# The start of an input projection in two halves of the contraction, a helper operation on another engine, and a common raster for operand tiles

## The chip, the cores and the metric

The kernel runs on one core of one Trainium2 chip. A core has the matrix engine TensorE (PE), VectorE (DVE), ScalarE (ACT) and GpSimd (POOL), and SyncE (SP), on whose queue nearly all transfers are issued. Each engine works through its own list of instructions in order and waits where an operand or a buffer isn't ready. Operands lie in SBUF, 128 partitions wide; products are summed in PSUM, here in eight banks of 128 x 512 float32. The metric is the device time of one execution in microseconds (us); lower is better. Times of single instructions are from one profiled execution.

## The reference

A trunk of two layers over 1024 tokens of width 1024, in float32. The part in which the change moves instructions is the first step of layer 0:

```python
def rmsnorm(x, g):
    return x * lax.rsqrt(jnp.mean(x * x, axis=-1, keepdims=True) + EPS) * g

def even_mixer(hn, w_in, w_conv, g_v, w_s, b_s, w_out):
    z = hn @ w_in                       # 1024 x 1024 by 1024 x 2560
    b_gate, c_gate, x_in, u, v = jnp.split(z, [512, 1024, 1536, 2048], axis=-1)
    y_a = short_gated_conv(b_gate, c_gate, x_in, w_conv)
    y_b = chunked_spatial_gating(u, v, g_v, w_s, b_s)   # gelu(v), normed, mixed in chunks of 128
    return jnp.concatenate([y_a, y_b], axis=-1) @ w_out
...
h = h + mixer(rmsnorm(h, g_mix))                        # layer 1: latent attention and mLSTM
h = h + (silu(hn @ w_gate) * (hn @ w_up)) @ w_down      # width 2816
h = h + sigmoid(rmsnorm(h, g_ple) @ w_ple_gate) * (p @ w_ple_proj)
```

## The kernel before

**Products.** Each float32 operand is split into a high part, rounded to the matrix engine's fast float32 type (a cast on ACT), and the low rest (a subtraction on DVE). `mm3` (L186) makes a product of two such pairs by three matmuls: high by high, high by low, low by high, at L189, L190 and L191. A matmul has weights (128 x 128, loaded ahead of it) and a moving operand of 512 columns. In the rows below a name as `zv<-hzva,x0h` reads: output, moving operand, weights; h and l are high and low part.

**The start.** `load_x(0)` (L363) puts the first 512 tokens of x on SP's queue as eight tiles `xt` of 256 KB: four token groups by two quarters q of the width. `x_group(n, q, kk)` (L878) transposes one group of 128 columns by four small matmuls into a product bank (`xT`) and splits it into `x0h`, `x0l`. At L922 all eight groups of the first token half are made. Then the weights `zv_unit` of the v columns come in two parts of the contraction, `zva` and `zvb`, four tiles each, scaled by the norm's gain while they are split (L149), then the second token half of x, and `x_scale(0)` (L899): eight squares on ACT with sums (`junk`), a reciprocal root in small DVE operations (L240 to L244), and `bcast_prep` (L278), which makes two diagonal matrices `dg`, one on DVE and one on POOL. `bcast` (L295) multiplies them by ones (L298, L299) and gives R, the scale by token, to be read from `ug` (L1037) on. It is put off by `later` until two products have passed; `tick` counts them.

The loop at L984 runs over the eight token tiles of 128: a `zv` product of 24 matmuls (contraction 1024 in eight steps of three), then, after tiles 0 to 3, two `x_group` of the second token half each, after tile 3 `x_scale(1)`, after tiles 4 and 5 the transposes `ws_T`, after tile 6 the first weights `uu` of the u columns, whose raw tiles `ru` POOL multiplies by the gain (L118). `v_done` (L932) makes gelu, squares on POOL (`gvs`), a norm in small DVE operations, and the split `vh`, `vl`. The products `pu`, `pm`, `pc`, `px` and `pb` follow.

**Banks.** `B.ps` (L80) hands out six product banks in turn, `B.ps_tr` (L83) two for transposes and the like; a bank can be written again when its last reader is done.

**Pools.** SBUF tiles come from pools: const; opB (operand slots below 32); w (raw weights `raw`, six buffers, and split weights `whi`, `wlo`, eight each); tmp; and, stacked behind them, opA (operand slots from 32, `slot`, L92), whose place other pools take later in the program. In the built program the operand tiles of opB and w start at byte 64 modulo 256 of a partition, those of opA at byte 192 modulo 256.

Which products have an operand in opA: x of the first layer lies there whole, so `zv`, `pu`, `pc`, `px` and `pb` have exactly one. In `ffn_up` (L484) the moving operands `xb` of products 1 and 2 lie in slots 0 to 15; those of products 3 to 7 (`xc`) are taken from the list at L452, slots 32 to 53 first, in the order of products 6, 7, 5, 4, 3. A column runs through its products in the order 1, 6, 2, 7, 5, 4, 3, each of four pairs, 12 matmuls. In the per-layer gate (`ppg`) the slots of the second token half (`X_SLOTS`, L653) lie in opA, those of the first don't. In the down projection (`pd`) all operands lie in opB and w.

Of the kernel before, what the change touches and what calls it, by code (L numbers as in the profile page):

```python
# [11 lines left out]
F32 = mybir.dt.float32  # L12
# [9 lines left out]
P = 128  # L22
T = 1024
D = 1024
KT = D // P
NT = T // P
HT = 512
# [12 lines left out]
RAW = 6  # L40
# [6 lines left out]
class Build:  # L47
# [59 lines left out]

    def w_part(self, srcs, kt, cols, name, gcol, slots=None):
        nc = self.nc
        raw = self.wp.tile([P, kt, cols], F32, tag="raw", name=self.name(f"r{name}"), bufs=RAW)  # L110
        o = 0
        for s in srcs:
            w = s.shape[1]
            nc.sync.dma_start(raw[:, :, o : o + w], s.rearrange("(k p) c -> p k c", p=P))
            o += w
        if gcol is not None and kt > 1:
            g = self.vec[:, gcol : gcol + kt].unsqueeze(2).to_broadcast([P, kt, cols])
            nc.gpsimd.tensor_tensor(out=raw, in0=raw, in1=g, op=ALU.mult)  # L118
        if slots:
            hi, lo = (  # L120
                self.slot(i, name=f"u{name}").rearrange("p (k c) -> p k c", k=kt) for i in slots
            )
        else:
            hi = self.wp.tile([P, kt, cols], F32R, tag="whi", name=self.name(f"h{name}"), bufs=8)
            lo = self.wp.tile([P, kt, cols], F32R, tag="wlo", name=self.name(f"l{name}"), bufs=8)
        if gcol is not None and kt == 1:
            self.split_scaled(hi, lo, raw, self.vec[:, gcol : gcol + 1])
        else:
            self.split(hi, lo, raw)
        return [(hi[:, k, :], lo[:, k, :]) for k in range(kt)]  # L130
# [23 lines left out]

    def w_quarter(self, w, rows, c, name):

        t = self.wp.tile([P, 4, P], F32, tag="raw", name=self.name(f"r{name}"), bufs=RAW)
        self.nc.sync.dma_start(
            t, w[rows * HT : (rows + 1) * HT, c].rearrange("(k p) c -> p k c", p=P)
        )  # L160
        return t
# [7 lines left out]
    def w_chain(self, w, c0, c1, name, eng):  # L169


        tt = eng.tensor_tensor
        raw = lambda: self.wp.tile([P, 4, P], F32, tag="raw", name=self.name(f"s{name}"), bufs=RAW)
        a11 = self.w_quarter(w, 0, c0, name)
        a21 = self.w_quarter(w, 0, c1, name)
        a22 = self.w_quarter(w, 1, c1, name)
        a12 = self.w_quarter(w, 1, c0, name)
        s1, s2 = raw(), raw()
        tt(out=s1, in0=a21, in1=a22, op=ALU.add)
        tt(out=s2, in0=s1, in1=a11, op=ALU.subtract)  # L180
        tt(out=a21, in0=a11, in1=a21, op=ALU.subtract)
        return {1: a11, 2: a12, 4: a22, 5: s1, 6: s2, 7: a21}
# [95 lines left out]
    def bcast_prep(self, r):  # L278

        nc = self.nc  # L280
        rh = self.tp.tile([P, 4], F32R, tag="rh", name=self.name("rh"), bufs=2)
        rl = self.small("rl", (P, 4))
        nc.vector.tensor_copy(rh, r)
        nc.vector.tensor_tensor(out=rl, in0=r, in1=rh.bitcast(F32), op=ALU.subtract)
        out = []
        for i, x in enumerate((rh.bitcast(F32), rl)):
            d = self.tmp("dg", (P, 4, P), F32R)
            (nc.vector, nc.gpsimd)[i].tensor_tensor(
                out=d, in0=self.ident.unsqueeze(1).to_broadcast([P, 4, P]),
                in1=x.unsqueeze(2).to_broadcast([P, 4, P]), op=ALU.mult,  # L290
            )
            out.append(d.rearrange("p a b -> p (a b)"))
        return out
# [31 lines left out]
def trunk(ctx, tc, x, p, positions, g_mix, g_ffn, g_ple, ev_w_in, ev_w_conv, ev_g_v, ev_w_s,  # L325
          ev_b_s, ev_w_out, od_w_in, od_b_gate, od_g_qa, od_g_kva, od_w_q_up, od_w_kv_up, od_g_q,
          od_g_k, od_g_mh, od_w_out, w_gate, w_up, w_down, w_ple_proj, w_ple_gate, out):
    nc = tc.nc
# [5 lines left out]
    bp = ctx.enter_context(tc.tile_pool(name="opB", bufs=1))  # L334
    dp = ctx.enter_context(tc.tile_pool(name="dram", bufs=1, space=DRAM))
    B.wp = ctx.enter_context(tc.tile_pool(name="w", bufs=1))
    B.tp = ctx.enter_context(tc.tile_pool(name="tmp", bufs=1))

    def open_ps():
        s = ExitStack()  # L340
# [11 lines left out]

    xt = {}

    def load_x(n):
        for q in range(2):
            for j in range(4):
                t = bp.tile([P, HT], F32, tag=f"bl{n}{q * 4 + j}", name=B.name("xt"))
                r = (n * 4 + j) * P
                nc.sync.dma_start(t, x[r : r + P, q * HT : (q + 1) * HT])  # L360
                xt[n, q, j] = t

    load_x(0)  # L363

    ident = cp.tile([P, P], F32, name="ident")
    make_identity(nc, ident)
# [290 lines left out]
    def ffn_down(l, act_d, h_d, h2_d, X2, st, normed):  # L657
# [6 lines left out]

        def part(fh, ch, f, t=None):
            if t is None:
                t = B.wp.tile([P, HT], F32, tag="raw", name=B.name("rd"), bufs=RAW)
            r = (fh * half + f) * P
            nc.sync.dma_start(t, w_down[l][r : r + P, ch * HT : (ch + 1) * HT])
            return t  # L670
# [163 lines left out]
    def ple_out(l, tok, h2_d, X, r):  # L834

        pT = {}
        for n in range(2):
            pT[n] = make_pT(load_p(l, n) if n else tok, [32 + 4 * n + i for i in range(4)])
        for cg in range(2):
            c = slice(cg * HT, (cg + 1) * HT)  # L840
            grp = B.tm_load(w_ple_gate[l], [(cg * HT, (cg + 1) * HT)], f"pg{cg}")
            hs = {}
            for n in range(2):
                for j in range(4):
                    t = hs[n, j] = B.slot(n * 4 + j + 8 * cg, F32, "h2")
                    nc.sync.dma_start(t, h2_d[n][cg * 4 + j])
            wj = []
            for k in range(2):
                raw = B.wp.tile([P, HT], F32, tag="raw", name=B.name("rpj"), bufs=RAW)
                nc.sync.dma_start(raw, w_ple_proj[l][k * P : (k + 1) * P, c])  # L850
                a = B.slots2(40 + 4 * cg + 2 * k, 41 + 4 * cg + 2 * k, "wj")
                B.split(a[0], a[1], raw)
                wj.append(a)
            for tt in range(NT):
                n, t = tt // 4, slice((tt % 4) * P, (tt % 4 + 1) * P)
                pg = B.tm_mm(grp, X, tt, "ppg")
                pj = B.ps("ppj")
                for k in range(2):
                    a = pT[n][k]
                    B.mm3(pj, (a[0][:, t], a[1][:, t]), wj[k], k == 0, k == 1)  # L860
                ph = B.ps_tr("ph")
                for j in range(4):
                    nc.tensor.transpose(ph[:, j * P : (j + 1) * P], hs[n, j][:, t], ident)
                s = B.tmp("psg")
                nc.scalar.activation(s, pg, AF.Sigmoid, scale=r[n][:, tt % 4 : tt % 4 + 1])
                nc.vector.tensor_tensor(out=s, in0=pj, in1=s, op=ALU.mult)
                nc.vector.tensor_tensor(out=s, in0=ph, in1=s, op=ALU.add)
                nc.sync.dma_start(out[tt * P : (tt + 1) * P, c], s)
# [30 lines left out]
    def x_scale(n):  # L899
        ss = B.small("ss", (P, 4, 2))  # L900
        for q in range(2):
            for j in range(4):
                junk = B.tmp("junk")
                nc.scalar.activation(
                    junk, xt[n, q, j], AF.Square, accum_out=ss[:, j, q : q + 1]
                )
        s4 = B.small("s4", (P, 4))
        nc.vector.tensor_tensor(out=s4, in0=ss[:, :, 0], in1=ss[:, :, 1], op=ALU.add)
        r = B.tp.tile([P, 4], F32, tag=f"rt{n}", name=B.name("rt"), bufs=2)
        B.tok_rms(s4, D, r)  # L910
        rtok[n] = r
        dg = B.bcast_prep(r)

        def fn():
            R[n] = B.bcast(n, dg)

        B.later(2, fn)

    pv = B.ps_tr("pvec", (P, 16))
    nc.tensor.transpose(pv, rows0, ident[0:16, 0:16])  # L920
    nc.vector.tensor_copy(vec[:, 0:16], pv)
    for q in range(2):  # L922
        for kk in range(4):
            x_group(0, q, kk)
    zv_unit = B.w_unit(w_in[0:512, 2048:2560], 4, HT, "zva", G_MIX)
    zv_unit += B.w_unit(w_in[512:1024, 2048:2560], 4, HT, "zvb", G_MIX + 4)
    load_x(1)
    x_scale(0)

    vch = {}  # L930

# [49 lines left out]
        w_in[:, 1536 + pr * P : 1536 + (pr + 1) * P], KT, P, f"u{pr}", G_MIX, slots  # L981
    )

    for tt in range(NT):  # L984
        ps = B.tm_mm((zv_unit, HT), X, tt, "zv")
        if tt == 1:
            pv = B.ps_tr("pvec", (P, 80))
            nc.tensor.transpose(pv, rows, ident[0:80, 0:80])
            nc.vector.tensor_copy(vec[:, 16:80], pv[:, 16:80])
        if tt < 4:  # L990
            for kk in range(2):
                x_group(1, tt // 2, (tt % 2) * 2 + kk)
            if tt == 3:
                x_scale(1)
        elif tt < 6:
            ws_T(tt - 4)
        elif tt == 6:
            u0 = u_unit(0, ((28, 29), (30, 31)))
        v_done(tt, ps)

# [241 lines left out]
    def up_weights(src, kt, cols, gcol, name):  # L1242
        pairs = []
        half = cols // 2
        for k in range(kt):
# [2 lines left out]
            )  # L1248
            for i in range(2):
                c = slice(i * half, (i + 1) * half)  # L1250
                raw = B.wp.tile([P, half], F32, tag="raw", name=B.name(f"r{name}"), bufs=RAW)
                nc.sync.dma_start(raw, src[k * P : (k + 1) * P, c])
                B.split_scaled(t[0][:, c], t[1][:, c], raw, col(gcol + k))
            pairs.append(t)
# [690 lines left out]
```

## Time and profile before

| what | value |
|---|---|
| time, median of 3 runs (lowest, highest) | 2453.76 us (2452.49, 2454.29) |
| profiled execution: its time, its span | 2453.51 us, 2451.8 us |
| busy in the span: PE, DVE, ACT, POOL | 98%, 64%, 40%, 28% |
| first `zv` product, first `pu` product start | 14.99 us, 73.39 us |

The span runs from the first to the last recorded instruction; 1.7 us of the execution's time lie around it. An engine's busy share says little of the end by itself: an idle stretch counts only where the matrix engine waits in it.

### The profile page before, as it was taken

What the parts mean: (1) busy time and instruction counts of PE and PEld (TensorE: products, weight loads), DVE (VectorE), ACT (ScalarE), POOL (GpSimd) and SP (SyncE); (2) the same over time, 40 slices, a digit from 0 to 9 for tenths busy, and PEclk for the clock granted to TensorE, in tenths of its full rate; (3) what the DMA queues carried; (4) which work ended last, traced back from release to release, by engine and by line L of the source; (5) the groups of instructions that cost most, each with busy time, mean ns of one, the idle gap of its engine ahead of it and who ended that gap; (6) DMA issues with size and microseconds to landing.
All of it is one profiled execution on the core that took longest, in us unless ns stands there. A gap on an engine that the chain in (4) does not pass through costs nothing.

```text
span 2451.8 us, 33875 instructions
## 1 busy us (share of the span) xinstructions
PE 2413.6 (98%) x11510; PEld 1993.8 (81%) x11510; DVE 1561.2 (64%) x3079; ACT 988.2 (40%) x1877; POOL 679.8 (28%) x678
## 2 busy tenths in 40 slices
PE   7999999999999999999999999999999999999999
PEld 6878887788888888888888788878788888888877
DVE  6864479645556778776785566548855455687731
ACT  5322244233233545444554455635333232454520
POOL 3452121546553000112321132111256556100000
PEclk9999999999999999999999999999999999999999
DMA  4221453433236966553454843154433233886721
GB/s 151 78 86 48 136 169 101 141 99 112 91 108 204 308 226 214 174 173 96 114 154 121 228 112 106 46 168 134 129 120 112 87 111 103 286 281 210 251 97 39
DMA packets 358685, 350.74 MB, mean 143 GB/s; under 512 B 24011, under 2 KB 249648, under 8 KB 358512
## 3 DMA queue, kind: packets, MB, share of 16 engines
q1 hardware_dynamic: 358016, 348.25, 45.3%
q8 instruction: 90, 1.47, 0.2%
q0 software_dynamic: 464, 0.33, 0.1%
q14 instruction: 83, 0.68, 0.1%
q10 hardware_dynamic: 32, 0.01, 0.0%
HBM read 255.18 MB, written 93.32 MB: 142 GB/s over the span
## 4 chain that ended last, share of the span: by engine, by line
PE 52%; DVE 4%; issue 2%; DMA 1%; ACT 1%; POOL 0%; SPq 0%; DVEq 0%; POOLq 0%; ACTq 0%
PE p L190 5%; PE p L189 5%; PE p L191 5%; PE pd L189 3%; PE pd L190 3%; PE pd L191 3%; PE O L1833 2%; PE ppg L191 2%; PE ppg L190 2%; PE ppg L189 2%; PE PT L1875 1%; PE po L189 1%; PE po L190 1%; PE po L191 1%; PE S L1775 1%
## 5 line engine op out<-in xcount | busy, mean ns | idle before, releaser
L189 PE MATMUL pd<-acth,hd 128*128 128x512 f32 x616 | 240.0, 390 | 0.1
L190 PE MATMUL pd<-actl,hd 128*128 128x512 f32 x616 | 239.7, 389 | 0.0
L191 PE MATMUL pd<-acth,ld 128*128 128x512 f32 x616 | 239.7, 389 | 0.0
L189 PE MATMUL p<-xch,hg 128*128 128x512 f32 x440 | 173.1, 394 | 5.3 <-DVE sg L534 2.2
L190 PE MATMUL p<-xcl,hg 128*128 128x512 f32 x440 | 173.1, 393 | 0.2
L189 PE MATMUL p<-xch,hu 128*128 128x512 f32 x440 | 173.0, 393 | 0.0
L191 PE MATMUL p<-xch,lu 128*128 128x512 f32 x440 | 172.9, 393 | 0.0
L191 PE MATMUL p<-xch,lg 128*128 128x512 f32 x440 | 172.9, 393 | 0.0
L190 PE MATMUL p<-xcl,hu 128*128 128x512 f32 x440 | 172.6, 392 | 0.0
L541 POOL TENSOR_TENSOR act<-act,sg 128x512 f32<-128x512 f32 x60 | 90.0, 1499 | 244.1 <-DVE act L534 239.3
L146 ACT CAST hu<-ru 128x512 fp32r<-128x512 f32 x116 | 71.6, 622 | 183.3 <-PE p L190 170.4
L189 PEld LDWEIGHTS pd<-acth,hd 128*128 128x128 f32 x616 | 115.6, 188 | 24.3 <-DVE res L728 0.5
L191 PEld LDWEIGHTS pd<-acth,ld 128*128 128x128 f32 x616 | 115.6, 188 | 24.3
L146 ACT CAST hg<-rg 128x512 fp32r<-128x512 f32 x110 | 68.2, 620 | 165.9 <-PE p L190 135.6
L190 PEld LDWEIGHTS pd<-actl,hd 128*128 128x128 f32 x616 | 115.6, 188 | 23.8
L147 DVE TENSOR_TENSOR lu<-ru,hu 128x512 fp32r<-128x512 f32 x116 | 117.2, 1011 | 14.9 <-ACT hu L146 14.9
L146 ACT CAST hd<-rd 128x512 fp32r<-128x512 f32 x110 | 68.3, 621 | 133.5 <-PE pd L190 82.2
L147 DVE TENSOR_TENSOR actl<-ra,acth 128x512 fp32r<-128x512 f32 x154 | 109.5, 712 | 12.1 <-ACT acth L146 12.0
L259 POOL TENSOR_TENSOR S<-S,sq 128x512 f32<-128x512 f32 x38 | 51.6, 1359 | 219.7 <-ACT sq L257 219.7
L147 DVE TENSOR_TENSOR ld<-rd,hd 128x512 fp32r<-128x512 f32 x110 | 76.9, 699 | 47.6 <-ACT hd L146 47.6
L189 PEld LDWEIGHTS p<-xch,hg 128*128 128x128 f32 x440 | 82.6, 188 | 26.5 <-ACT hg L146 3.0
L146 ACT CAST acth<-ra 128x512 fp32r<-128x512 f32 x154 | 94.7, 616 | 13.1 <-DMA ra<-act 9.3
(561 smaller groups left out, 6615.9 us busy)
## 6 DMA issues: line engine op xcount, KB each, us to landing
ra<-act SPq DMA_DIRECT2D x154, 256.0 KB, 3.7
rd<-in_w_down SPq DMA_DIRECT2D x154, 256.0 KB, 4.0
rg<-in_w_gate SPq DMA_DIRECT2D x100, 256.0 KB, 3.3
ru<-in_w_up SPq DMA_DIRECT2D x100, 256.0 KB, 2.9
act<-act SPq DMA_DIRECT2D x88, 256.0 KB, 2.0
act<-at SPq DMA_DIRECT2D x66, 256.0 KB, 2.0
rpg<-in_w_ple_gate SPq DMA_DIRECT2D x48, 256.0 KB, 3.0
sd<-in_w_down SPq DMA_DIRECT2D x44, 256.0 KB, 4.2
```

What stands on the lines that cost most here:

```text
L146: self.nc.scalar.copy(hi, src)
L147: (eng or self.nc.vector).tensor_tensor(out=lo, in0=src, in1=hi.bitcast(F32), op=ALU.subtract)
L189: mm(ps, a[0], b[0], start=first, stop=False, skip_group_check=more)
L190: mm(ps, a[0], b[1], start=False, stop=False, skip_group_check=more)
L191: mm(ps, a[1], b[0], start=False, stop=last, skip_group_check=more)
L259: eng.tensor_tensor(out=st[n], in0=st[n], in1=sq, op=ALU.add)
L541: (nc.vector if last else nc.gpsimd).tensor_tensor(out=t, in0=t, in1=sg[d["i"], key], op=ALU.mult)
L1775: mm(s[:, 0:w], q0, K0[:, c0 : c0 + w], start=True, stop=False)
L1833: nc.tensor.matmul(O[h][:, b * DV : (b + 1) * DV], t[:, j * P : (j + 1) * P], V[h // 2][:, kb, (h % 2) * DV : (h % 2 + 1) * DV], start=kb ...
L1875: nc.tensor.transpose(pt[:, j * P : (j + 1) * P], e[:, j * P : (j + 1) * P], ident)
```

## The change

Three things. First, x and the first weights are loaded in quarters and the first products are made in two parts. `load_x` takes the quarters to load; the queue gets the first quarter of x, `zva`, the second quarter, `zvb`. Four product banks are opened at once, and for token tiles 0 to 3 the first half of the contraction (12 matmuls) is made before the second; the transposes of x's second quarter stand after the first halves of tiles 1 and 2. `x_scale(0)` comes behind the first halves, and R four products later instead of two. The transposes of the second token half stand, four groups each, after tiles 1 and 2 instead of two groups after each of tiles 0 to 3; `ws_T` and the first u weights come one tile later. Second, both diagonals of `bcast_prep` are made by DVE; there are ten calls in the program. Third, the raw tiles get a pool of their own, and this and tmp are put on the right side of SBUF. In the built program the operand tiles of opA then start at byte 64 modulo 256, as those of opB and w, which stay at 64.

```diff
-    B.tp = ctx.enter_context(tc.tile_pool(name="tmp", bufs=1))
+    B.rp = ctx.enter_context(tc.tile_pool(name="raw", bufs=1, side="right"))
+    B.tp = ctx.enter_context(tc.tile_pool(name="tmp", bufs=1, side="right"))
...
-        raw = self.wp.tile([P, kt, cols], F32, tag="raw", name=self.name(f"r{name}"), bufs=RAW)
+        raw = self.rp.tile([P, kt, cols], F32, tag="raw", name=self.name(f"r{name}"), bufs=RAW)
...
-        for i, x in enumerate((rh.bitcast(F32), rl)):
+        for x in (rh.bitcast(F32), rl):
             d = self.tmp("dg", (P, 4, P), F32R)
-            (nc.vector, nc.gpsimd)[i].tensor_tensor(
+            nc.vector.tensor_tensor(
...
-    def load_x(n):
-        for q in range(2):
+    def load_x(n, qs=(0, 1)):
+        for q in qs:
...
-    load_x(0)
+    load_x(0, (0,))
...
-        B.later(2, fn)
+        B.later(4, fn)
...
-    for q in range(2):
-        for kk in range(4):
-            x_group(0, q, kk)
+    for kk in range(4):
+        x_group(0, 0, kk)
     zv_unit = B.w_unit(w_in[0:512, 2048:2560], 4, HT, "zva", G_MIX)
+    load_x(0, (1,))
     zv_unit += B.w_unit(w_in[512:1024, 2048:2560], 4, HT, "zvb", G_MIX + 4)
     load_x(1)
-    x_scale(0)
...
+    def zv_half(ps, tt, q):
+        c = slice(tt * P, (tt + 1) * P)
+        for k in range(4 * q, 4 * q + 4):
+            a = X[0][k]
+            B.mm3(ps, (a[0][:, c], a[1][:, c]), zv_unit[k], k == 0, k == KT - 1)
+
+    zv = [B.ps("zv") for _ in range(4)]
+    for tt in range(4):
+        zv_half(zv[tt], tt, 0)
+        if tt in (1, 2):
+            for kk in range(2):
+                x_group(0, 1, 2 * tt - 2 + kk)
+    x_scale(0)
     for tt in range(NT):
-        ps = B.tm_mm((zv_unit, HT), X, tt, "zv")
+        if tt < 4:
+            ps = zv[tt]
+            zv_half(ps, tt, 1)
+            B.tick()
+        else:
+            ps = B.tm_mm((zv_unit, HT), X, tt, "zv")
...
         if tt < 4:
-            for kk in range(2):
-                x_group(1, tt // 2, (tt % 2) * 2 + kk)
+            if tt in (1, 2):
+                for kk in range(4):
+                    x_group(1, tt - 1, kk)
             if tt == 3:
                 x_scale(1)
-        elif tt < 6:
-            ws_T(tt - 4)
-        elif tt == 6:
+        elif tt < 7:
+            if tt > 4:
+                ws_T(tt - 5)
+        else:
             u0 = u_unit(0, ((28, 29), (30, 31)))
```

The queue of SP from its fourth transfer on (`xt` is a tile of x, `rzva` and `rzvb` raw weights). Before:

```order
L360 DMA xt_81<-in_x 128x512
L360 DMA xt_83<-in_x 128x512
L360 DMA xt_85<-in_x 128x512
L360 DMA xt_87<-in_x 128x512
L360 DMA xt_89<-in_x 128x512
L114 DMA rzva_52_204<-in_ev_w_in 128x512
L114 DMA rzva_55_210<-in_ev_w_in 128x512
```

The same queue in the changed kernel:

```order
L361 DMA xt_84<-in_x 128x512
L114 DMA rzva_36_163<-in_ev_w_in 128x512
L114 DMA rzva_39_169<-in_ev_w_in 128x512
L114 DMA rzva_42_175<-in_ev_w_in 128x512
L114 DMA rzva_45_181<-in_ev_w_in 128x512
L361 DMA xt_187<-in_x 128x512
L361 DMA xt_189<-in_x 128x512
```

The four transfers of `zva` have moved ahead of the second four tiles of x.

ACT's list around its first split operands (`junk` is a square, `x0h` a cast of x, `hzva` a scaled cast of weights). Before:

```order
L904 ACTIVATE junk_281,ss_268<-xt_87 128x512
L904 ACTIVATE junk_283,ss_268<-xt_89 128x512
L146 CAST x0h_137<-xT_132 128x512
L150 ACTIVATE hzva_53_206<-rzva_52_204,vec 128x512
L146 CAST x0h_146<-xT_141 128x512
L150 ACTIVATE hzva_56_212<-rzva_55_210,vec 128x512
```

In the changed kernel, from the second square on:

```order
L905 ACTIVATE junk_345,ss_342<-xt_80 128x512
L905 ACTIVATE junk_347,ss_342<-xt_82 128x512
L905 ACTIVATE junk_349,ss_342<-xt_84 128x512
L150 ACTIVATE hzva_37_165<-rzva_36_163,vec 128x512
L150 ACTIVATE hzva_40_171<-rzva_39_169,vec 128x512
L146 CAST x0h_132<-xT_127 128x512
L150 ACTIVATE hzva_43_177<-rzva_42_175,vec 128x512
L146 CAST x0h_141<-xT_136 128x512
```

Four squares instead of eight stand ahead of the first split operands; the other four come behind those of `zva`.

ACT's list further on, in the changed kernel, where the transposes of the second token half are split (`gv` is the gelu of a `zv` product, 254 and 255 those of tiles 0 and 1; `uu` a cast of u weights that POOL has multiplied):

```order
L934 ACTIVATE gv_112_396<-zv_254,rt_361 128x512
L146 CAST uu_0_214_851<-ru_0_213_848 128x512
L146 CAST uu_4_217_858<-ru_4_216_855 128x512
L934 ACTIVATE gv_132_472<-zv_255,rt_361 128x512
L146 CAST x0h_441<-xT_436 128x512
L146 CAST x0h_450<-xT_445 128x512
L146 CAST x0h_459<-xT_454 128x512
L146 CAST x0h_468<-xT_463 128x512
```

Before, this stretch reads:

```order
L146 CAST x0h_359<-xT_354 128x512
L146 CAST x0h_368<-xT_363 128x512
L934 ACT_TABLE_LOAD
L934 ACTIVATE gv_115_372<-zv_329,rt_287 128x512
L934 ACTIVATE gv_132_448<-zv_397,rt_287 128x512
L301 COPY R_425<-Rb_422 128x512
L146 CAST x0h_435<-xT_430 128x512
L146 CAST x0h_444<-xT_439 128x512
L146 CAST uu_0_206_798<-ru_0_205_795 128x512
```

The two `uu` casts have moved ahead of tile 1's gelu, and the splits of the second token half, two by two before, come in a block of four behind both.

## Rows read from the trace of the kernel before

**Rows 1.** The page: busy us (share of the span) and instructions, first line.
```profile
PE 2413.6 (98%) x11510; PEld 1993.8 (81%) x11510; DVE 1561.2 (64%) x3079; ACT 988.2 (40%) x1877; POOL 679.8 (28%) x678
```
**Rows 2.** Waits of PE, whole span: who for whom, us in total, times, longest.
```profile
PE zv L189 <- ACT x0h L146: 4.0, 1, 4.0
...
PE pm L189 <- DVE ug L1037: 1.7, 1, 1.7
...
PE Rb L299 <- POOL dg L288: 1.5, 4, 0.4
...
PE pc L189 <- DVE yb L1017: 0.6, 1, 0.6
```
**Rows 3.** Timeline of PE, start: start us, us, instructions [idle before <-releaser].
```profile
14.99 0.80 PE L189 MATMUL zv<-hzva,x0h 128*128 128x512 f32 x1 [0.60 <-DVE x0l L147]
...
17.72 0.47 PE L882 MATMUL xT<-ident,xt 128*128 128x128 f32 x2
...
20.52 0.44 PE L882 MATMUL xT<-ident,xt 128*128 128x128 f32 x2 [0.94 <-DMA xt<-in_x]
...
36.61 1.03 PE L882 MATMUL xT<-ident,xt 128*128 128x128 f32 x8
...
52.30 0.80 PE L189 MATMUL zv<-hzvb,x0h 128*128 128x512 f32 x1 [4.01 <-ACT x0h L146]
...
55.19 0.73 PE L977 MATMUL wst<-ident,wsr 128*128 128x128 f32 x4
...
73.39 0.40 PE L189 MATMUL pu<-x0h,uu 128*128 128x512 f32 x1
```
**Rows 4.** Timeline of ACT, start.
```profile
8.40 0.63 ACT L904 ACTIVATE junk<-xt 128x512 f32<-128x512 f32 x1 [0.47 <-DMA xt<-in_x]
...
11.11 0.57 ACT L146 CAST x0h<-xT 128x512 fp32r<-128x512 f32 x1
11.57 0.72 ACT L150 ACTIVATE hzva<-rzva,vec 128x512 fp32r<-128x512 f32 x1
...
33.45 0.63 ACT L146 CAST uu<-ru 128x512 fp32r<-128x512 f32 x1 [1.35 <-POOL ru L118]
```
**Rows 5.** Timeline of POOL, start.
```profile
32.38 6.04 POOL L118 TENSOR_TENSOR ru<-ru,vec 128x512 f32<-128x512 f32 x6
```
**Rows 6.** Timeline of DVE, 52 to 135 us: one small operation twice.
```profile
79.52 0.16 DVE L240 SCALAR_TENSOR_TENSOR rqw<-rqy 128x8 f32<-128x8 f32 x1
...
81.93 0.97 DVE L240 SCALAR_TENSOR_TENSOR rqw<-rqy 128x8 f32<-128x8 f32 x1
```
**Rows 7.** Stretches: us, busy (instructions) of PE, PEld, DVE, ACT, POOL; PEclk, DMA share, GB/s.
```profile
40.00:75.00 35.00, 30.99 (x135) 24.57 (x134) 29.28 (x99) 14.41 (x33) 8.53 (x9) 0.95 0.06 16
75.00:140.00 65.00, 62.73 (x316) 52.44 (x315) 57.01 (x96) 19.10 (x33) 34.53 (x27) 1.00 0.33 106
...
780.00:980.00 200.00, 200.00 (x882) 165.35 (x882) 158.92 (x253) 99.96 (x177) 6.31 (x4) 1.00 0.76 254
```
**Rows 8.** Timeline of PE: first matmuls of products 7, 5, 4 and 3 of one column.
```profile
601.93 0.40 PE L189 MATMUL p<-xch,hg 128*128 128x512 f32 x1
...
604.72 0.40 PE L189 MATMUL p<-xch,hg 128*128 128x512 f32 x1
...
607.52 0.40 PE L189 MATMUL p<-xch,hg 128*128 128x512 f32 x1
...
610.25 0.39 PE L189 MATMUL p<-xch,hg 128*128 128x512 f32 x1
```
**Rows 9.** Timeline of PE: first matmuls of a `pb` product and, two products later, of `pc`.
```profile
154.62 0.40 PE L189 MATMUL pb<-x0h,hb 128*128 128x512 f32 x1
...
165.78 0.39 PE L189 MATMUL pc<-x0h,hc 128*128 128x512 f32 x1
```
**Rows 10.** Line L288, whole span: duration ns min/median/max, first and last start us.
```profile
L288 DVE TENSOR_TENSOR dg<-ident,rh x10: 679/684/686, 27.9 to 1688.7; 128x512 fp32r<-128x512 f32 x10
L288 POOL TENSOR_TENSOR dg<-ident,rl x10: 1279/1367/1422, 28.2 to 1688.8; 128x512 fp32r<-128x512 f32 x10
```

More of the change, by code (lines that the diff above doesn't have):

```diff
@@ L155, in w_quarter @@
     def w_quarter(self, w, rows, c, name):
-        t = self.wp.tile([P, 4, P], F32, tag="raw", name=self.name(f"r{name}"), bufs=RAW)
+        t = self.rp.tile([P, 4, P], F32, tag="raw", name=self.name(f"r{name}"), bufs=RAW)
         self.nc.sync.dma_start(
@@ L172, in w_chain @@
         tt = eng.tensor_tensor
-        raw = lambda: self.wp.tile([P, 4, P], F32, tag="raw", name=self.name(f"s{name}"), bufs=RAW)
+        raw = lambda: self.rp.tile([P, 4, P], F32, tag="raw", name=self.name(f"s{name}"), bufs=RAW)
         a11 = self.w_quarter(w, 0, c0, name)
@@ L666, in part @@
             if t is None:
-                t = B.wp.tile([P, HT], F32, tag="raw", name=B.name("rd"), bufs=RAW)
+                t = B.rp.tile([P, HT], F32, tag="raw", name=B.name("rd"), bufs=RAW)
             r = (fh * half + f) * P
@@ L848, in ple_out @@
             for k in range(2):
-                raw = B.wp.tile([P, HT], F32, tag="raw", name=B.name("rpj"), bufs=RAW)
+                raw = B.rp.tile([P, HT], F32, tag="raw", name=B.name("rpj"), bufs=RAW)
                 nc.sync.dma_start(raw, w_ple_proj[l][k * P : (k + 1) * P, c])
@@ L1250, in up_weights @@
                 c = slice(i * half, (i + 1) * half)
-                raw = B.wp.tile([P, half], F32, tag="raw", name=B.name(f"r{name}"), bufs=RAW)
+                raw = B.rp.tile([P, half], F32, tag="raw", name=B.name(f"r{name}"), bufs=RAW)
                 nc.sync.dma_start(raw, src[k * P : (k + 1) * P, c])
```

## The prediction

> **What bounds the kernel now.** I began with the busy time of the page: TensorE is busy 98% of the span [rows 1], so a change moves the time only where it shortens TensorE's own instructions or one of its few waits. Next I read TensorE's list of waits [rows 2]. After the first stage hardly any is over 2 us; the largest that this change can touch is the 4.0 us of a `zv` product for an operand that ScalarE (ACT) splits late. Then I read the start by the timeline [rows 3]: the first product of the input projection starts at 14.99 us, the `zv` stage ends where `pu` begins, at 73.39. The busy times by stretch [rows 7] show who else could be the bound: in 75 to 140 us VectorE (DVE) works 57.0 of 65 us, TensorE 62.7, and there TensorE waits twice for DVE (1.7 for `ug`, 0.6 for `yb` [rows 2]). From 140 us on TensorE is alone.
>
> Last I compared products of equal shape, since a 98% busy engine gains only from faster instructions. In the gate and up products (`p`) a product is 12 matmuls, and its length is the distance of its first start from that of the next. Between 601.93 and 604.72 stands product 7, whose moving operand lies in opA: 2.79 us. Between 607.52 and 610.25 stands product 4, moving operand in opB: 2.73 us, same shape, same weights' pool [rows 8]. So a matmul costs 232.5 ns with an operand in opA and 227.5 without; I use 5.0 ns as the price. Two more views agree: `pb` to `pc` is two products of 24 with x in opA, 11.16/48 = 232.5 ns [rows 9]; 200 us of `pd`, whose operands lie in opB and w alone, hold 882 records, 226.8 ns each [rows 7]. In the built program what sets opA apart is its place: its tiles start at byte 192 of a 256-byte raster, those of opB and w at 64. I take the distance of the two operands on that raster to be the cause, not the pool; no row here settles that (rival A).
>
> **Part one, the pools.** With raw and tmp on the right, the tiles of opA, opB and w all start at byte 64 of that raster; the distance between moving operand and weights becomes 0 everywhere. By the code the 512-column matmuls with exactly one operand in opA are:
> - `p`: 12 of the 28 operand pairs of one gate or up column lie in opA, times 3 matmuls, times 44 columns = 1584, at 5.0 ns 7.9 us.
> - `ppg`: the second half of the tokens in both layers, some 390: 2.0 us.
> - `pc`, `px`, `pb`: 24 products of 24 = 576: 2.9 us.
> - `ppj`: about 113: 0.6 us.
> - `pu` 192 and `zv` 182: 0.9 us each. That of `zv` goes into the next part; that of `pu` I count as nothing, since DVE shares the bound there.
>
> Sum: 13.4 us, all on the path, since TensorE waits for nothing in these stages. No work is added: the tiles are as many and as large. What DVE and ACT pay for reading raw and tmp at other addresses no row shows; as nothing in those stages waits for them I take 0, and 1 us either way for the range. From rounding (0.01 us in a difference of 0.06) the price is 4.2 to 5.8 ns: 11 to 15.5 us.
>
> What the Trainium skill says speaks against this part: "SBUF — State Buffer", section "Who interferes with whom", gives TensorE two independent read ports, one for the moving operand and one for the weights, and has it wait for no other engine. By that, operand distance would cost nothing, the 13.4 would be 0, and the time would come out as in rival A below; rows 8 speak for the price.
>
> **Part two, the start.** Now the queue of SP sends eight tiles of x, then `zva`. The fifth tile is there at about 8.3 (ACT's square of it waits until 8.40 [rows 4]). In the changed kernel that place in the queue is `zva`'s first part, and x's second quarter comes four places later. ACT then splits `zva` at 0.72 and x at 0.57 each [rows 4], no longer behind eight squares: the operands of the first matmul are done at about 10.3 instead of 14.99, a gain of 4.7.
>
> From there I count work. From 14.99 to 73.39 lie 58.4 us. Idle in it are 0.9 (at 20.52) and 4.0 (at 52.30) [rows 3]. Twice the clock stood at its lower level, 1.2 GHz: 14.99 to 17.72 held 6 matmuls in 2.73 us, 52.30 to 55.19 again 6 in 2.89 [rows 3]; six take 1.4 at 2.4 GHz, so the two cost 1.3 and 1.5; both follow TensorE's idleness, and the granted clock of 40 to 75 us is 0.95 [rows 7]. Work at full clock: 58.4 - 4.9 - 2.8 = 50.7. Added are 16 transposes of x's second quarter, which stood before 14.99: eight are busy for 1.03, overlapping (at 36.61) [rows 3], so about 0.8 each time, 1.6. Taken away is the 0.9 of `zv`. That leaves 51.4.
>
> What is late next: the first halves need eight splits, each a cast on ACT (0.5 to 0.63 apart) and a subtraction on DVE (0.6 to 0.7 apart), and the last is done at about 14.2. So the first 12 matmuls take 3.9 instead of 2.8, and run at the lower clock as now: 1.1 + 1.3. Then the banks. Four of the six product banks stay open, so the transposes of the second token half take turns in two, and the third and fourth group need the banks of tile 0 and 1. Tile 1's is free after ACT's `gv` of it, which stands behind two `uu` casts, and these wait for GpSimd (POOL): they waited 1.35 for it (at 33.45) [rows 4], and POOL does six such multiplications in 6.0 us without a pause [rows 5]. I work out 1.2 us there. The next four groups need banks whose `x0l` subtractions stand in DVE's queue behind tile 0's small operations; while POOL multiplies, such an operation takes 0.97 us for 0.16 [rows 6]: 2.0 us. The 4.0 us wait goes, because both groups of four are split ahead of ACT's second set of squares. For a further stretch at the lower clock after one of these waits I add 0.7, half of one. Sum: 10.3 + 51.4 + 2.4 + 3.2 + 0.7 = 68.0 instead of 73.39: **5.4 us gained**. Without bank waits and the second slow stretch it is 9, with waits twice as long and a whole slow stretch 1.5.
>
> Does it last beyond 75 us? DVE's chain there starts with the last `zv` tile, and POOL's multiplications, which it waits for, come when DVE frees raw tiles; both move with TensorE. So the waits of 1.7 and 0.6 stay as long and come earlier. That R is broadcast two products later costs nothing: its first reader is `ug` after the first `pu` product.
>
> **Part three, the second diagonal.** Ten times it leaves POOL, where it takes 1.28 to 1.42 us, for DVE, where its twin takes 0.68 [rows 10]. DVE had been done with the first when POOL was still at it, so L299's operand comes some 0.3 to 0.5 us sooner. TensorE's waits there sum to 1.5 [rows 2]; I take 0.7 of it, range 0 to 1.5. DVE gets 6.8 us more work in all, most where it isn't late. The queue behind it: rsqrt operations of the next tile, 0.6 us later, at two places in the first 75 us; that is inside the range of part two.
>
> The Trainium skill's page "SBUF — State Buffer", in the same section, lets a DVE instruction with two SBUF inputs contend with a GpSimd one that reads SBUF; rows 6 agree (0.97 for 0.16). The diagonal on DVE has two such inputs; by that rule some of the ten would last as long as POOL's, and this part would give 0 for 0.7.
>
> **Sum.** 13.4 + 5.4 + 0.7 = 19.5 us. The profiled execution took 2453.51 us, 0.2 below the median; 2453.5 - 19.5 = **2434.0 us** (0.8% less). About 0.2%, 4.9 us, is what a measurement of this kernel can tell from no change.
>
> **Rivals.**
> - *A, placement does nothing.* The 5 ns could belong to opA's own region or to what else runs in those stages, not to the distance. For it: nothing but opA's products shows it, and I have no run with another distance. Against: one column of `p` shows both times within 8 us, under the same load. Then only parts two and three stay: 2453.5 - 6.1 = 2447.4. Chance 0.13.
> - *B, the start gives its gain back.* The banks and POOL's multiplications take what the earlier start gives (waits of 8 us instead of 3.2, or DVE falls behind by as much in 75 to 140 us, where it has 8 us of slack in 65). For it: rows 5 to 7. Against: the second groups' splits stand ahead of the squares now. Then 2453.5 - 13.4 - 0.7 = 2439.4. Chance 0.15.
> - *C, slower.* The held banks: eight transposes groups, each freed only after a cast on ACT and a subtraction on DVE, behind POOL's 6.0 us of multiplications, twice. It becomes a loss when the two waits exceed the gain, 5.4 + 3.2 = 8.6 us, and A holds too; with a wait of 6.0 for each bank pair and the clock falling after both (1.5 each), 15 us against 8.6: 2453.5 + 6.4 - 0.7 = 2459. Against: half of `ru`'s multiplications have no reader before `pu`. Chance 0.04.
> - My forecast: 0.68.
>
> **How the numbers follow.** Ends of the forecast's terms: 15.5 + 9 + 1.5 + 1 gives 2426.5, 11 + 1.5 - 1 gives 2442. B lies inside. A is 2445 to 2452 by the range of the start. To leave out no more than 2 in 10 I take 2427 to 2445; outside are A, C and the tails. Faster by over 0.2% (below 2448.9): the forecast, B and two thirds of A, 0.92. Within: the last third of A, some of C, 0.05. Slower: 0.03.
>
> **What would show it.** Product 7 of a `p` column as long as product 4, 2.73 us; two products from `pb` to `pc` 10.9 instead of 11.16; `pd`'s 226.8 ns unchanged. First `zv` matmul at about 10.3, first `pu` at about 68; no 4.0 us wait for `x0h`, but waits of 1 to 2 us of the second half's transposes. L299 waiting for DVE, under 1 us in all. The forecast is wrong if the 2.79 stays, if `pu` starts after 72, or if `pd` gets longer.

## The result, and the profile after

The changed kernel takes 2436.70 us (median of 4 runs, 2436.30 to 2441.11) against 2453.69 (4 runs): ratio 0.9935, 95% interval 0.9918 to 0.9953. That is 17.0 us or 0.7% faster; forecast were 2434.0 us and 2427 to 2445. Run again, it stood at 0.9923 (0.9909 to 0.9937) of before. The profiled execution took 2437.04 us, its span 2435.3.

What answers to [rows 1] and [rows 2], the busy line of the page and the first of TensorE's waits over the whole span:

```profile
PE 2393.7 (98%) x11502; PEld 1993.3 (82%) x11510; DVE 1555.8 (64%) x3089; ACT 988.1 (41%) x1877; POOL 671.9 (28%) x668
```

```profile
PE pm L189 <- DVE ug L1057: 5.8, 2, 3.1
PE p L189 <- DVE u L595: 4.1, 2, 2.1
PE S L1795 <- DMA Q<-qTd: 3.6, 1, 3.6
...
PE xT L883 <- DVE x0l L147: 2.3, 2, 1.8
...
PE xT L883 <- ACT gv L934: 1.4, 1, 1.4
```

TensorE is busy 19.9 us less, at the same number of matmuls (8 records are missing). The 4.0 us wait for `x0h` has shrunk to 0.2. The two bank waits that the prediction worked out at 1.2 and 2.0 us stand there with 1.4 and 2.3. New is the first row: `pm` now waits 5.8 us, in two places, for what was 1.7 in one. In the profile of the repeat it is less:

```profile
PE pm L189 <- DVE ug L1057: 3.9, 2, 2.0
```

The wait for the second diagonal has no row any more. The list of [rows 2] counts there the idle time of the matmuls alone. The view of line L299 adds that of the weight loads ahead of them; before, and in the changed kernel, it reads:

```profile
  POOL dg L288: 5.3, 10
```

```profile
  DVE dg L288: 1.3, 5
```

The start, as in [rows 3], by the timeline of TensorE:

```profile
10.19 0.70 PE L189 MATMUL zv<-hzva,x0h 128*128 128x512 f32 x1 [0.24 <-ACT x0h L146]
...
32.44 0.66 PE L883 MATMUL xT<-ident,xt 128*128 128x128 f32 x4 [1.37 <-ACT gv L934]
...
37.62 2.00 PE L883 MATMUL xT<-ident,xt 128*128 128x128 f32 x12 [1.76 <-DVE x0l L147]
...
67.11 0.39 PE L189 MATMUL pu<-x0h,uu 128*128 128x512 f32 x1
```

The first product starts at 10.19 us, `pu` at 67.11 instead of 73.39: 6.3 us are gained by then. The products in which a matmul was dear, as in [rows 8] and [rows 9]: first the start of product 7 of a gate column and, four products or 48 matmuls later, of the next column; then `pc` and, 48 matmuls later, `px`:

```profile
593.83 0.39 PE L189 MATMUL p<-xch,hg 128*128 128x512 f32 x1
...
604.71 0.39 PE L189 MATMUL p<-xbh,hu 128*128 128x512 f32 x1
```

```profile
163.69 0.39 PE L189 MATMUL pc<-x0h,hc 128*128 128x512 f32 x1
...
174.57 0.39 PE L189 MATMUL px<-x0h,hx 128*128 128x512 f32 x1
```

Both take 10.88 us, 226.7 ns a matmul; two products of [rows 9] took 11.16. What answers to [rows 7], by stretch:

```profile
40.00:75.00 35.00, 34.83 (x159) 28.85 (x160) 32.45 (x111) 19.15 (x42) 8.25 (x9) 1.00 0.10 29
75.00:140.00 65.00, 58.55 (x295) 49.72 (x294) 54.85 (x91) 15.16 (x26) 38.82 (x29) 0.97 0.32 103
...
780.00:980.00 200.00, 199.86 (x886) 165.35 (x886) 158.00 (x262) 98.13 (x175) 5.02 (x3) 1.00 0.76 249
```

In 40 to 75 us TensorE is now busy nearly throughout, at full clock. In 75 to 140 it is busy 58.6 us where it was 62.7, and the mean granted clock is 0.97. The control is `pd`, in the last row, whose stretch now also takes in what follows it. By their starts two of its matmuls lie 226.8 ns apart before and 226.7 after: it is unchanged.

Read against each other, the starts of the same matmuls in both timelines tell where the time went (us). The last column has them from the profile of the repeat:

| product | before | after | after less before | repeat |
|---|---|---|---|---|
| first `pu` | 73.39 | 67.11 | -6.3 | 67.34 |
| first `pc` | 132.25 | 129.36 | -2.9 | 127.62 |
| first `px` | 143.47 | 141.93 | -1.5 | 139.72 |
| last `pb` group | 255.02 | 250.73 | -4.3 | 248.52 |
| first `p`, layer 0 | 355.01 | 350.14 | -4.9 | 347.92 |
| `pd`, layer 0 | 787.11 | 776.42 | -10.7 | 775.92 |
| `ppj`, second token half | 1092.72 | 1079.70 | -13.0 | 1079.45 |
| first `p`, layer 1 | 1681.81 | 1671.42 | -10.4 | 1671.05 |
| `pd`, layer 1 | 2113.73 | 2098.29 | -15.4 | 2097.27 |
| last `ppj` | 2445.30 | 2428.86 | -16.4 | 2427.06 |

Between `pu` and `px` the start's gain falls from 6.3 to 1.5 us here and from 6.1 to 3.8 in the repeat, so two executions of one kernel differ by over 2 us in this loss. The stages with dear matmuls then bring their gain one after another. The attention in between gives some 3 us back. TensorE's wait for Q's transfer is 3.6 us for 1.7, and behind it the granted clock is lower; six matmuls there start 0.42 us apart instead of 0.23:

```profile
1366.00:1378.00 12.00, 10.00 (x44) 7.82 (x46) 5.36 (x11) 3.41 (x10) 0.77 (x1) 0.86 1.03 238
```

### The profile page after: what moved, and what is told of

Same layout as the page of the kernel before. It is cut to its first block, busy times and chain, and to the rows that moved or that the text cites. A ratio compares the mean times of both kernels' runs of the same rounds, so it can differ in the third digit from the quotient of the medians.

```text
span 2435.3 us, 33878 instructions
## 1 busy us (share of the span) xinstructions
PE 2393.7 (98%) x11502; PEld 1993.3 (82%) x11510; DVE 1555.8 (64%) x3089; ACT 988.1 (41%) x1877; POOL 671.9 (28%) x668
## 4 chain that ended last, share of the span: by engine, by line
PE 87%; DVE 7%; DMA 2%; issue 2%; ACT 1%; POOL 0%; SPq 0%; DVEq 0%; POOLq 0%; ACTq 0%
PE p L189 10%; PE p L190 10%; PE p L191 10%; PE pd L189 6%; PE pd L190 5%; PE pd L191 5%; PE po L189 2%; PE po L190 2%; PE po L191 2%; PE O L1853 2%; PE ppg L191 2%; PE ppg L190 2%; PE ppg L189 2%; PE PT L1895 1%; PE S L1795 1%
## 5 line engine op out<-in xcount | busy, mean ns | idle before, releaser
L146 ACT CAST acth<-ra 128x512 fp32r<-128x512 f32 x154 | 94.7, 616 | 14.5 <-DMA ra<-act 10.7
```

What stands on the lines that cost most here:

```text
L146: self.nc.scalar.copy(hi, src)
```

## The experiments

All ratios are to the kernel before on the same chip; there its times were some 2 to 3 us higher and more spread than in the runs above.

**A gap alone.** Kernel before. A smaller tile of ones makes 256 bytes of room, and a gap of 128 bytes ahead of opA takes half of it, so that on the 256-byte raster only opA, and the pools that later take its place, move.

```diff
-    ones_f = cp.tile([P, P], F32, name="ones_f")
+    ones_f = cp.tile([P, 64], F32, name="ones_f")
...
+    gap = ctx.enter_context(tc.tile_pool(name="gap", bufs=1)).tile([P, 32], F32, name="gap")
+    nc.gpsimd.memset(gap, 0.0)
```

> The kernel before, with one thing changed: a gap of 128 bytes ahead of opA (room for it is made by a smaller tile of ones), so that opA's operand tiles start at byte 64 modulo 256 like those of opB and w. No pool moves otherwise, no instruction of the products changes. Distance theory: product 7 of a p column takes as long as product 4 (2.73 us instead of 2.79), two products from pb to pc take 10.9 instead of 11.16, and the time falls by the 13.4 us of the prediction's first part to about 2440 us. Rival (opA's region or the pools on the right are the cause): 2.79 and 11.16 stay and the time stays at 2453.7 us.

Measured: 2442.82 us, ratio 0.9947 (0.9933 to 0.9960). The stretch of 150 to 250 us, where `pc`, `px` and `pb` stand, holds, in the kernel before and with the gap:

```profile
150.00:250.00 100.00, 100.00 (x432) 81.08 (x431) 41.38 (x58) 19.24 (x30) 29.18 (x26) 1.00 0.18 52
```
```profile
150.00:250.00 100.00, 100.00 (x443) 82.81 (x442) 40.75 (x60) 19.99 (x31) 28.38 (x25) 1.00 0.17 49
```

Such a count takes in the matmuls that only reach into the stretch. Of the 432, 430 start in it, 232.4 ns from start to start; of the 443 it is 441, 226.7 ns apart. The 128 bytes bring the gain, and no instruction of the products had to move for it.

**The pools alone.** Kernel before with raw and tmp on the right (the lines on `B.rp` and `B.tp` of the diff).

> The kernel before with the third part alone: raw and tmp on the right. Distance theory: the same as with the gap alone, about 2440 us, within 2 us of it. If reading raw and tmp at other addresses costs or gains something for VectorE and ScalarE, the two differ by more than that.

Measured: 2441.31 us, 0.9938 (0.9925 to 0.9951), again 443 records in that stretch. The two runs agree within their intervals: the new pools bring no more than the gap does, and reading raw and tmp elsewhere shows no price of its own.

**The changed kernel with the distance put back.** The same gap in the changed kernel, which takes opA off the raster.

> The changed kernel with a gap of 128 bytes ahead of opA, so that its tiles are 128 bytes off the raster of opB and w again. Distance theory: product 7 takes 2.79 us again, two products from pb to pc 11.16, and the time is 14 us more than the changed kernel. Rival (the move of raw and tmp is what gains): nothing changes.

Measured: 2452.89 us, 0.9988 (0.9979 to 0.9998), beside 2436.33 of the changed kernel on the same chip, 16.6 us more. The stretch:

```profile
150.00:250.00 100.00, 100.00 (x432) 81.09 (x431) 41.04 (x57) 19.26 (x30) 26.55 (x24) 1.00 0.17 48
```

Back to 432, and 232.4 ns. So all but some 3 us of the change's gain hang on 128 bytes.

**The changed kernel again**, the partner of three runs on that chip.

> The changed kernel as it is, beside the next three on the same chip: 0.993 to 0.994 of the time of before.

Measured: 2436.33 us, 0.9923 (0.9909 to 0.9937).

**The start alone.** The changed kernel with the old pools and the second diagonal on GpSimd.

> The changed kernel with the old pools and the old diagonal on GpSimd: the first part (quarters and halves) alone. Theory: pu starts at about 68 to 69 us instead of 73.4, but 3 to 5 us of it are lost in waits of pm for the chain of the last v tile, as in the changed kernel (5.8 us of such waits there); time 2450 to 2452 us. Rival (the chain is slow because the second diagonal went to VectorE): the waits of pm stay at about 2 us and the time is 2447 to 2448 us.

Measured: 2453.60 us, 0.9990 (0.9981 to 0.9999): 2.5 us, at the edge of what shows. `pu` starts at 68.87, 4.5 us early; the first `pc` at 130.36, 1.9 early. In time the theory holds (it had 1.7 to 3.7 us less than before), but not in its cause: TensorE's waits of `pm` sum to 2.5 us, near the rival's 2, yet the gain went all the same. From `pu` to `pc` it is 2.6 us longer than before. Of that 0.8 are in these waits. The granted clock of 75 to 140 us is 0.97 here for 1.00 before, which makes some 2 us of 65 (an estimate from these two numbers):

```profile
75.00:140.00 65.00, 61.88 (x305) 51.59 (x304) 57.56 (x98) 16.42 (x28) 37.44 (x29) 0.97 0.34 107
```

**The diagonals alone.** Kernel before with both on DVE.

> The kernel before with the second part alone: both diagonals on VectorE. Forecast of the prediction: 0.7 us less, 2453.0 us. Rival: the 0.6 us more on VectorE ahead of the last v tile lengthens the waits of pm by as much, no gain, 2453.7 to 2455 us.

Measured: 2451.57 us, 0.9977 (0.9968 to 0.9986): 5.6 us less, eight times the forecast, and both expectations missed. The waits of TensorE up to 140 us:

```profile
PE zv L189 <- ACT x0h L146: 2.3, 1, 2.3
...
PE pm L189 <- DVE ug L1037: 0.7, 1, 0.7
```

The wait for `x0h` fell from 4.0 to 2.3 and that of `pm` from 1.7 to 0.7; the first `pc` starts 3.0 us earlier. On POOL the diagonal stood ahead of the `gvs` squares and the `ru` multiplications. Without its 1.35 us the six `ru` start at 31.43 where they started at 32.38 [rows 5], and the DVE chain behind them isn't slowed for as long:

```profile
31.43 6.21 POOL L118 TENSOR_TENSOR ru<-ru,vec 128x512 f32<-128x512 f32 x6
```

The rest is gained at L299 after all. Taken from the start of one matmul to that of the thirtieth behind it, the stretches around the ten pairs of L298 and L299 are 2.8 us shorter in all than in the kernel before. At six of the ten, all after 300 us, it is 0.3 to 0.7 us each. Together these are 5.8 us for the 5.6 measured. The profiled execution was the slowest of eleven (2455.67 us) and lost its gain again elsewhere, so the profile shows these places and not the sum.

**The changed kernel with the second diagonal back on GpSimd.**

> The changed kernel with the second diagonal back on GpSimd. If moving it gains by shortening GpSimd's queue ahead of the gvs and ru operations (theory now, since alone it took some 5 us from the kernel before, where a 4.0 us wait for x0h stood behind that queue): in the changed kernel that wait is gone already, so little is left, 0 to 2 us more than the changed kernel. Rival (diagonals on VectorE lengthen the chain of the v tiles, whose pm wait is 5.8 us there): the wait falls to about 2.5 us and the time is 2 to 3 us less than the changed kernel.

Measured: 2436.28 us, 0.9919 (0.9906 to 0.9932), by its time the same as the changed kernel. The intervals leave room for some 3 us either way, though. In the traces the stretches around L299 are 2.9 us longer than in the changed kernel, at the same six places. What would offset them isn't shown; the clock of 75 to 140 us was 1.00 in this one profile and 0.97 in those of the changed kernel. The wait for `x0h`, which the diagonals shortened alone, is gone in both, and the waits of `pm` are 5.9 us for 5.8: on both waits that it shortened alone, the step brings nothing any more.

**The squares of the v tiles on ScalarE.** In the changed kernel:

```diff
-        nc.gpsimd.tensor_tensor(out=sq, in0=g, in1=g, op=ALU.mult)
+        nc.scalar.activation(sq, g, AF.Square)
```

> The changed kernel with the eight squares gvs of the v tiles on ScalarE instead of GpSimd. Theory (the chain of the last v tile is late because its square on GpSimd stands behind the rc multiplication, which waits for its transfer until 74.95 us): the sum of the last tile starts at about 74 us instead of 77.9, the wait of pm of 3.1 us at 94 goes, the time is 3 to 5 us less than the changed kernel. Rival (VectorE's own work sets the end of the chain): the wait shrinks by less than 1 us and the time stays.

Measured: 2428.73 us, 0.9888 (0.9874 to 0.9902), 7.6 us less than the changed kernel and the fastest of all. In the changed kernel POOL's timeline has, ahead of the last tile's square (the row at 76.84), a multiplication that waits 7.4 us for its transfer, and DVE sums that square at 77.91 and makes the last `vl` at 92.88:

```profile
74.95 1.93 POOL L118 TENSOR_TENSOR rc<-rc,vec 128x512 f32<-128x512 f32 x1 [7.43 <-DMA rc<-in_ev_w_in]
76.84 1.04 POOL L939 TENSOR_TENSOR gvs<-gv 128x512 f32<-128x512 f32 x1
```

```profile
77.91 0.69 DVE L941 TENSOR_REDUCE v<-gvs 128x8 f32<-128x512 f32 x1 [1.01 <-POOL gvs L939]
...
92.88 0.69 DVE L147 TENSOR_TENSOR vl<-gv,vh 128x512 fp32r<-128x512 f32 x1 [0.74 <-ACT vh L146]
...
121.88 1.99 DVE L1037 SCALAR_TENSOR_TENSOR yb<-pm,vec,bias 64x256 f32<-64x256 f32 x4 [2.59 <-DMA xT<-xk]
```

With the squares on ScalarE the same two DVE steps:

```profile
71.84 0.67 DVE L941 TENSOR_REDUCE v<-gvs 128x8 f32<-128x512 f32 x1
...
85.35 0.69 DVE L147 TENSOR_TENSOR vl<-gv,vh 128x512 fp32r<-128x512 f32 x1 [0.69 <-ACT vh L146]
```

The chain ends 7.5 us sooner: 6.1 lie ahead of the sum (1.9 of them before `pu`, which starts at 65.26), 1.5 behind it. Both waits of `pm` are gone from TensorE's list: 3.1 us at 94.32, behind that chain, and 2.75 at 127.77, behind the `yb` above, where DVE waits 2.6 for a transfer. The theory stands; it gave more than expected because the later wait went as well, and the granted clock of 75 to 140 us is 1.00 again. Without the squares POOL also works beside DVE for less time; the run doesn't part this from the squares' place in the queue.

**The same without the first part.** Old start, with the pools, the diagonals and these squares.

> The kernel before with the pools, the diagonals and the squares on ScalarE, but without the first part (quarters and halves): what the start is worth once the chain of the v tiles is short. Theory: the start's whole gain now shows, 4 to 6 us more than with the first part, 2433 to 2435 us. Rival (most of the 4.0 us wait for x0h came from GpSimd's queue and goes by the diagonals and squares alone): 0 to 2 us more, 2429 to 2431 us.

Measured: 2431.89 us, 0.9902 (0.9883 to 0.9922). The interval overlaps that of the kernel with the new start, so the times alone don't settle what the start is worth there. In the profiles `pu` starts at 68.71 without it and 65.26 with it, the first `pc` at 125.30 and 121.41: 3.5 to 3.9 us, between the two expectations, and not lost by `pc`.

The start of the first `pc` in all these kernels (from their timelines, us):

| kernel | first `pu` | first `pc` | from the one to the other |
|---|---|---|---|
| before | 73.39 | 132.25 | 58.9 |
| start alone | 68.87 | 130.36 | 61.5 |
| diagonals alone | 71.33 | 129.27 | 57.9 |
| changed | 67.11 | 129.36 | 62.3 |
| changed, repeat | 67.34 | 127.62 | 60.3 |
| squares on ACT, old start | 68.71 | 125.30 | 56.6 |
| squares on ACT, changed | 65.26 | 121.41 | 56.2 |

With the squares on POOL the stretch between them grows when `pu` is earlier by the new start: by 2.6 of 4.5 us, by 3.4 of 6.3, and in the repeat by 1.4 of 6.1. These are single profiles, and two of one kernel differ by 2.0. With the squares on ACT it is 56.2 to 56.6 whichever the start.

**Other distances.** The gap of the third experiment with 64, 192 and 32 bytes.

> The changed kernel with opA's tiles 64 bytes off the raster of opB and w. Either only the distance of 128 bytes is slow (two products from pb to pc 10.88 us, time as the changed kernel), or every distance but 0 costs (11.16 us and 16 us more), or something between.

> The same with 192 bytes. If the cost depends on the distance modulo 128, this is as the run with 64; if it has a direction (moving operand ahead of or behind the weights), the two differ.

> The changed kernel with opA's tiles 32 bytes off the raster. Two products from pb to pc (48 matmuls, moving operand 32 bytes further than the weights) take 10.88 us if only distances of 64 bytes and more cost, about 10.93 if the cost grows evenly with the distance (64 bytes: 10.99).

Measured: 2450.18 us, 0.9977 (0.9966 to 0.9987) with 64; 2449.99, 0.9970 (0.9958 to 0.9983) with 192; 2452.97, 0.9984 (0.9972 to 0.9996) with 32. The stretch of 150 to 250 us, in that order:

```profile
150.00:250.00 100.00, 100.00 (x439) 82.05 (x438) 40.46 (x59) 19.26 (x30) 28.98 (x25) 1.00 0.17 48
```
```profile
150.00:250.00 100.00, 100.00 (x430) 80.55 (x430) 40.44 (x58) 19.17 (x30) 26.09 (x24) 1.00 0.17 48
```
```profile
150.00:250.00 100.00, 100.00 (x430) 80.34 (x429) 40.38 (x59) 19.26 (x30) 26.29 (x24) 1.00 0.17 48
```

By the starts, with the moving operand 64 bytes further than the weights a matmul takes 228.9 ns, with 192 it takes 233.3, and with 32 also 233.3. So neither expectation on evenness holds: every distance tried but 0 costs, +64 least in these products. That the direction counts shows in `zv`, where the operand in opA is the weights and not the moving one. First `zv` and `pu` with 64 bytes (47 matmuls of `zv` from the first row to the second, 71 of `pu` from the third to the fourth), then with 192:

```profile
43.77 0.39 PE L189 MATMUL zv<-hzva,x0h 128*128 128x512 f32 x1
...
54.73 0.39 PE L191 MATMUL zv<-hzvb,x0l 128*128 128x512 f32 x1
...
67.51 0.40 PE L189 MATMUL pu<-x0h,uu 128*128 128x512 f32 x1
...
83.77 0.39 PE L191 MATMUL pu<-x0h,lu 128*128 128x512 f32 x1
```
```profile
43.70 0.39 PE L189 MATMUL zv<-hzva,x0h 128*128 128x512 f32 x1
...
54.47 0.39 PE L191 MATMUL zv<-hzvb,x0l 128*128 128x512 f32 x1
...
67.06 0.39 PE L189 MATMUL pu<-x0h,uu 128*128 128x512 f32 x1
...
83.62 0.40 PE L191 MATMUL pu<-x0h,lu 128*128 128x512 f32 x1
```

With 64 bytes `zv` takes 233.2 ns a matmul and `pu` 229.0; with 192 it is 229.1 and 233.2. So the cost isn't that of opA's byte by itself. In all these runs opB and w stay at byte 64, though: that each role has a dear byte of its own isn't excluded, since no run moves both operands.

The time with 64 is hardly better than with 128. The starts of products 1, 6, 2 and 7 of one `p` column in that kernel:

```profile
588.02 0.40 PE L189 MATMUL p<-xbh,hg 128*128 128x512 f32 x1
...
590.79 0.40 PE L189 MATMUL p<-xch,hg 128*128 128x512 f32 x1
...
593.55 0.40 PE L189 MATMUL p<-xbh,hg 128*128 128x512 f32 x1
...
596.32 0.40 PE L189 MATMUL p<-xch,hg 128*128 128x512 f32 x1
```

The first three take 2.76 or 2.77 us, 230 to 231 ns a matmul, products 1 and 2 as well, whose operands both lie on the raster (2.72 in the changed kernel). So the distance of a matmul's own two operands isn't the whole of it: what stands before or beside it counts too. No run here tells which.

## Why the prediction was right, and where it wasn't

**The pools: right in mechanism, undersized.** The price read from [rows 8] was 5.0 ns a matmul. By the starts in `pc`, `px` and `pb` it is 232.4 - 226.7 = 5.7. The term that was mis-sized most is `p`, because product 4 was taken as free of the cost. Over all columns the four products with both operands on the raster took 2.74 to 2.75 us on the mean before and 2.72 to 2.73 after, so they were dearer too beside the others. The matmuls of `p` in 100 us, before and after:

```profile
600.00:700.00 100.00, 100.00 (x437) 81.58 (x436) 19.51 (x29) 4.68 (x8) 1.00 0.33 103
```
```profile
600.00:700.00 100.00, 100.00 (x443) 82.82 (x442) 20.21 (x30) 4.08 (x7) 1.00 0.32 99
```

By all their starts at full clock they went from 230.1 to 226.8 ns. For the 3696 matmuls of both layers that is some 12 us, where the forecast had 7.9. With 3.3 of `pc`, `px` and `pb`, 2.0 of `ppg` and 0.8 of `ppj` the matmuls give some 18 us for the 13.4 of the sum, more than its range of 15.5. Not all of it reaches the time: 13.0 and 15.2 us were measured alone and 16.6 in the changed kernel, each with `zv` and `pu` included. "TensorE waits for nothing in these stages" was too simple. Its waits in `p` sum to 7.7 us after and 6.1 before, and the attention gives some 3 us back. Rival A has fallen: the 5 ns don't belong to opA's region, since they go with a gap of 128 bytes and come back with it. The Trainium skill's "SBUF — State Buffer", section "Who interferes with whom", has moving operand and weights on independent read ports; the runs show that where the two lie against each other costs up to 6.6 ns all the same, and the measurement decides.

**The start: right to 75 us, wrong after.** First matmul 10.3 forecast, 10.19 found; `pu` 68.0 and 67.11; bank waits 1.2 and 2.0, found 1.4 and 2.3. The step that failed is "does it last beyond 75 us?": it said that POOL's multiplications and DVE's chain move with TensorE and the waits of `pm` stay. They didn't stay, 5.8 us for 1.7, and with the lower clock that followed (0.97 in 75 to 140 us) 4.7 us of the 6.3 were gone by the first `px`, in the repeat 2.3 of 6.1. The square of the last v tile stands on POOL behind a multiplication that waits for its transfer, and that transfer waits on SP's queue for raw tiles that DVE frees. This was so before too, and the chain had next to no slack. Its sum and its last `vl` then:

```profile
82.91 0.69 DVE L941 TENSOR_REDUCE v<-gvs 128x8 f32<-128x512 f32 x1
...
96.21 0.69 DVE L147 TENSOR_TENSOR vl<-gv,vh 128x512 fp32r<-128x512 f32 x1 [0.74 <-ACT vh L146]
```

The sum moved by 5.0 us (to 77.91) and the last `vl` by 3.3 (to 92.88), where TensorE moved by 6.3: 1.3 us were lost ahead of the sum and 1.7 behind it. That is rival B in its second form, in size as well in the one profile (4.7 of 5.4), less so in the other. The run with the squares on ScalarE shows that the squares on POOL cause it: there the waits are gone.

**The diagonals: mechanism right, undersized, and a second effect overlooked.** 0.7 us were taken from the waits at L299, with 1.5 as the most. That 1.5 is what the matmuls waited; with the weight loads it was 5.3, and it fell to 1.3. Around these places 2.8 to 2.9 us were gained, whether the step came alone or into the changed kernel. Alone the step brought 5.6 us (3.4 to 7.9), the rest by POOL's queue: the prediction looked at who waits for the diagonal and not at what stands behind it on POOL. The ten moved diagonals take 0.67 to 1.53 us on DVE; the longest, at 55.94, lies beside a POOL multiplication. That agrees with what the Trainium skill's "SBUF — State Buffer" says, in the same section, of a DVE instruction with two SBUF inputs beside a GpSimd one that reads SBUF; for most of the ten it didn't matter (median 0.68).

```profile
L288 DVE TENSOR_TENSOR dg<-ident,rl x10: 674/684/1531, 25.3 to 1678.9; 128x512 fp32r<-128x512 f32 x10
```

**The sum.** 13.4 + 5.4 + 0.7 = 19.5 was forecast, 17.0 measured. By the traces the matmuls gave some 18 us and the diagonals 2.9; of the start 1.5 were left, and 1.6 in `p` and some 3 in the attention were lost again, 18 in all. That the forecast came so near is in part luck: two terms were too small, one too large, and two losses were missing. The loss in the attention, where Q's transfers end later than TensorE needs them, is read from the profiles and wasn't tested; the run with the pools alone shows it too (a wait of 2.5 us).

## What to carry to other kernels

Read the price of a matmul by its operands' tiles even where the engine is 98% busy: equal shapes at 226.7 and 232.4 ns were 13 to 17 us here, and a gap of 128 bytes in the layout brings them without moving an instruction. An engine that starts earlier gains only as far as the next chain has slack; follow the operand that is needed latest through every queue it passes, POOL's among them, before booking the gain. When a step leaves an engine, look at what stood behind it there as well as at who waited for it, and count the waits of the weight loads with those of the matmuls.

## What the hardware showed that was not expected

The start-to-start time of 128 x 512 float32 matmuls depends on where moving operand and weights lie against each other in a partition: 226.7 ns at the same byte of the 256-byte raster, 233.3 with the moving operand 32 bytes further, 228.9 at 64, 232.4 at 128 and 233.3 at 192 (100 us of `pc`, `px`, `pb` each, full clock; the weights stay at byte 64). With the roles exchanged, in `zv`, 64 and 192 change places. With 64 bytes neighbouring products on the raster slowed as well (230 to 231 ns for 226.7). Which law lies behind these numbers stays open.
